# A two-layer decoder trunk on one core: up groups of the MLP in pairs, by seven block products

## The chip, the cores and the metric

The kernel runs on one core of a Trainium2 chip, in one launch. What counts is device time in microseconds (us). A time before is given as the median of three runs; the profile is a further execution, with its own time. In the profile PE is TensorE's matmuls and PEld its weight loads, DVE is VectorE, ACT ScalarE, POOL GpSimd, SP SyncE. DMAs are issued here from SP (plain loads and stores) and from POOL (loads that add to what the tile already holds, called accumulates below).

## The reference

512 tokens of width 1024 go through two layers; each has a mixer (gated linear attention in the first, stick-breaking attention in the second) and an MLP. The change concerns the MLP, whose inner width is 4096:

```python
def sq_relu_mlp(x, w_up, w_down):
    h = jax.nn.relu(x @ w_up)
    return (h * h) @ w_down

h = layer_norm(DEEPNORM_ALPHA * h + mix, ln_g[layer, 0], ln_b[layer, 0])
h = layer_norm(DEEPNORM_ALPHA * h + sq_relu_mlp(h, mlp_w_up[layer], mlp_w_down[layer]),
               ln_g[layer, 1], ln_b[layer, 1])
```

Everything is float32, in and out.

## The kernel before

**Products.** A float32 operand is split into hi and lo, two tiles of the type fp32r: hi is a copy made by ACT, lo is the operand less hi, made by the DVE (`split_tile`, L70 and L72, for weights; `put`, L98 and L99, for tokens). A product is three matmuls, hi by hi, hi by lo and lo by hi (`mm3`, L93 to L95; in the block products, L347).

**Up.** The inner width is cut into eight groups of 512. `up(g)` (L689) takes 512 of them: the weights are the stationary operand (128x128), the tokens move, 512 columns at a time, 4 banks of PSUM by 8 parts of the contraction by three, 96 matmuls. `up(0)` alone moves its tokens in two halves of 256. Its weights come in four raw pieces (512 KB each) from SP, and each piece is split. After that ACT takes the relu (L702) and the DVE (L704) or ACT (L706) the square, into a tile s2 of which there are three.

**Down.** `seven` (L292) multiplies two up groups (512 tokens by 1024) with 1024 by 1024 of the down weights, by seven block products of 2x2 blocks in place of eight. Each product takes 256 tokens, in two parts of 128 that are the stationary operand, with 12 matmuls of 512 moving columns for each part; seven products make 168. Sums and differences of blocks are needed on both sides:

- weights: four blocks in two halves each, eight tiles B (128x1024, eight buffers). b12 and b22 are sums of two blocks: a load by SP (L312), then an accumulate by POOL (L306). Two later sums, of b11 and b22 (the third), then of b21 and that (the fourth), are made by the DVE on the tiles (L371, L381), or, with `ends`, by more accumulates. Such a tile is split when a product needs it (`split_b`); the fifth product's weights come as raw pieces (`plain_b`).
- tokens: differences of blocks on the DVE, each split by `split_a`.

The products' results are added to the residual rows h by the DVE (L164, L168). The order of a down: first (b11), second (b21), third (b12), fourth (b11 with the third sum), then the product of the plain block, the seventh (b22), and the last (b21 with the fourth sum).

**Order.** `mlp` (L677) writes it by hand: up(0), up(1), affine, up(2), down(0), up(3), up(4), down(2), up(5), up(6), down(4), up(7), down(6). A scheduler then orders the rows of each engine, by its own estimates; on the chip every engine runs its rows in that order and waits where one is not ready. `affine` (L190) applies the layer norm's gain and shift to the four rows h: 16 operations of 128x512 on the DVE. A load into a tile waits until the last reader of its buffer is done; for a B tile that is the DVE's lo. There are six hi and six lo tiles for weights, three raw, and eight token units T.

Of the kernel before, what the change touches and what calls it, by code (L numbers as in the profile page):

```python
# [34 lines left out]
def yoco_kernel(ctx: ExitStack, tc: tile.TileContext, x, gla_w_in, gla_w_a2, gla_b_a, gla_norm_g,  # L35
# [22 lines left out]
    def unit(dtype):  # L58
        return big.tile([P, 4, 512], dtype, tag="T", bufs=8, name=nm("T"))
# [7 lines left out]
    def split_tile(raw, a):  # L67
        v = lambda w: w.rearrange("p (a b) -> p a b", a=a)
        hi = wts.tile([P, 1024], F32R, tag="hi", bufs=6, name=nm("hi"))
        nc.scalar.activation(hi, raw, AF.Copy)  # L70
        lo = wts.tile([P, 1024], F32R, tag="lo", bufs=6, name=nm("lo"))
# [66 lines left out]
    def lnvec(l, i):  # L138
        g = const.tile([P, D], F32, tag="lng", name=nm("lng"))
        b = const.tile([P, D], F32, tag="lnb", name=nm("lnb"))  # L140
# [144 lines left out]
    def ahead(a1, seventh=True):  # L285

        s1, s2 = (lambda u: (u[:, :, 0:256], u[:, :, 256:512]))(unit(F32))
        first = split_a(a1[:, :, 0:256])
        nc.vector.tensor_tensor(s2, a1[:, :, 0:256], a1[:, :, 256:512], op=ALU.subtract)
        return s1, s2, first, split_a(s2) if seventh else None  # L290

    def seven(a1, a2, weights, pool, hs, fresh, norms=(), mid=None, ends=False, begun=None):  # L292

# [8 lines left out]
        bs = []  # L302

        def more(b, h, k, j):

            nc.gpsimd.dma_start(out=b.rearrange("p (a b) -> p a b", a=2), in_=weights(k, h, j), accum_op=ALU.add)  # L306

        for h in range(2):
            four_b = []
            for k, j, other in ((1, 1, (0, 1)), (0, 1, (0, 0)), (0, 0, None), (1, 0, None)):  # L310
                b = pool.tile([P, 1024], F32, tag="B", bufs=8, name=nm("B"))
                nc.sync.dma_start(out=b.rearrange("p (a b) -> p a b", a=2), in_=weights(k, h, j))  # L312
                if other:
                    more(b, h, *other)
                four_b.append(b)
            bs.append(four_b)

        def split_b(i):
            got = []
            for h in range(2):  # L320
                hi, lo = split_tile(bs[h][i], 2)
                got += [(hi[:, 0, :], lo[:, 0, :]), (hi[:, 1, :], lo[:, 1, :])]
            return got

        def plain_b(k, j):
            got = []
# [647 lines left out]
```

## Time and profile before

| | |
|---|---|
| median of 3 runs | 1121.65 us (1121.54 to 1121.96) |
| profiled execution, its own time | 1122.18 us |
| its span on the core | 1120.3 us |
| granted TensorE clock, mean | 0.999 |
| one up group (512 columns) | 21.75 us (two in 43.5) |
| one down | 38.1 us (365.1 to 403.2) |
| last down, first and second layer | 40.9 us and 38.3 us |
| MLP of layer 0 | 214.5 to 547.5 us of the span |
| MLP of layer 1 | 781.7 to 1110.9 us of the span |

A row of a group reads: line, engine, operation, output from inputs by the program's names, shapes, count, then busy time in us and mean ns of one, then the idle time of that engine just before such rows. A row of the timeline starts with the start and the duration, both in us. Matmuls overlap, so that the distance of their starts, and not their duration, is what one costs. "To landing" is the time from a DMA's issue until its data are there.

### The profile page before, as it was taken

How to read it: one execution, taken by the hardware profiler on the slowest of the kernel's cores; microseconds unless marked ns; L12 is line 12 of the kernel's file. 1: busy time of each engine (PE TensorE's matmuls, PEld its weight loads, DVE VectorE, ACT ScalarE, POOL GpSimd, SP SyncE). 2: the span in 40 equal slices, each digit the busy share in tenths (PEclk: the TensorE clock that was granted, in tenths of full speed). 3: DMA queues.
4: the chain of work that ended last, by engine and by line, in shares of the span. 5: the costliest groups of instructions: out<-in, count | busy, mean ns of one | idle time of the engine just before them, and what ended most of it. 6: DMA issues, size and time to landing. Idle time of an engine off the chain costs nothing.

```text
span 1120.3 us, 14346 instructions
## 1 busy us (share of the span) xinstructions
PE 1112.0 (99%) x5519; PEld 920.9 (82%) x5519; DVE 803.9 (72%) x981; ACT 551.0 (49%) x829; POOL 168.2 (15%) x199
## 2 busy tenths in 40 slices
PE   9999999999999999999999999999999999999997
PEld 7888888898888888888888777778988888888885
DVE  4577639986856856848945888887677767667677
ACT  4455437653533534535634666664445435336353
POOL 1011222110100100122200434330200000001131
PEclk9999999999999999999999999999999999999999
DMA  8442399492670760786344221211965716706784
GB/s 248 121 132 57 117 257 215 133 285 85 189 206 25 205 202 19 204 203 137 113 113 132 57 76 39 76 38 38 295 194 149 223 42 166 229 19 187 172 133 91
DMA packets 105368, 157.52 MB, mean 141 GB/s; under 512 B 12306, under 2 KB 37266, under 8 KB 105300
## 3 DMA queue, kind: packets, MB, share of 16 engines
q1 hardware_dynamic: 87060, 120.96, 33.5%
q0 software_dynamic: 18240, 35.66, 18.6%
q8 instruction: 43, 0.70, 0.3%
q14 instruction: 25, 0.20, 0.1%
HBM read 153.45 MB, written 3.15 MB: 140 GB/s over the span
## 4 chain that ended last, share of the span: by engine, by line
PE 94%; DVE 4%; POOL 1%; issue 1%; POOLq 0%; DVEq 0%
PE ps L347 29%; PE ps L93 19%; PE ps L94 19%; PE ps L95 19%; PE ps L846 2%; PE ps L832 2%; PE ps L795 2%; POOL rs L184 1%; DVE lo L72 1%; DVE h L194 1%; DVE h L168 1%; DVE bst L175 1%; DVE T L99 0%; PE ps L567 0%; PE ps L121 0%
## 5 line engine op out<-in xcount | busy, mean ns | idle before, releaser
L347 PE MATMUL ps<-hi,T 128*128 128x512 f32 x1008 | 313.2, 390 | 0.0
L93 PE MATMUL ps<-T,hi 128*128 128x512 f32 (+1 forms) x768 | 288.5, 376 | 0.0
L94 PE MATMUL ps<-T,hi 128*128 128x512 f32 (+1 forms) x768 | 285.7, 372 | 0.1
L95 PE MATMUL ps<-T,lo 128*128 128x512 f32 (+1 forms) x768 | 285.4, 372 | 0.0
L72 DVE TENSOR_TENSOR lo<-raw,hi 128x1024 fp32r<-128x1024 f32 x134 | 162.9, 1219 | 122.8 <-ACT hi L70 122.2
L70 ACT ACTIVATE hi<-raw 128x1024 fp32r<-128x1024 f32 x134 | 141.9, 1063 | 175.7 <-PE ps L94 62.7
L347 PEld LDWEIGHTS ps<-hi,T 128*128 128x128 f32 x1008 | 188.9, 188 | 39.9 <-DVE T L99 1.0
L72 DVE TENSOR_TENSOR lo<-B,hi 128x1024 fp32r<-128x1024 f32 x108 | 131.1, 1221 | 99.8 <-ACT hi L70 99.7
L347 PE MATMUL ps<-lo,T 128*128 128x512 f32 x504 | 196.2, 389 | 0.0
L70 ACT ACTIVATE hi<-B 128x1024 fp32r<-128x1024 f32 x108 | 114.2, 1059 | 162.1 <-PE ps L94 106.3
L95 PEld LDWEIGHTS ps<-T,lo 128*128 128x128 f32 x768 | 144.7, 188 | 25.2
L93 PEld LDWEIGHTS ps<-T,hi 128*128 128x128 f32 x768 | 144.6, 188 | 24.5 <-issue 0.9
L94 PEld LDWEIGHTS ps<-T,hi 128*128 128x128 f32 x768 | 144.8, 189 | 23.9 <-DVE T L99 0.3
L306 POOL DMA_DIRECT2D B<-in_mlp_w_down_dram x52 | 62.4, 1234 | 540.9 <-DMA B<-in_mlp_w_down_dram 451.6
L347 PEld LDWEIGHTS ps<-lo,T 128*128 128x128 f32 x504 | 94.7, 188 | 19.5
L93 PE MATMUL ps<-hi,T 128*128 128x512 f32 x256 | 102.3, 400 | 0.0
L95 PE MATMUL ps<-hi,T 128*128 128x512 f32 x256 | 100.1, 391 | 0.0
L94 PE MATMUL ps<-lo,T 128*128 128x512 f32 x256 | 100.1, 391 | 0.0
L168 DVE TENSOR_TENSOR h<-h,ps 128x512 f32<-128x512 f32 x110 | 74.7, 680 | 6.0 <-PE ps L95 3.6
L823 POOL TENSOR_TENSOR w<-w,r 128x512 f32<-128x512 f32 x32 | 53.0, 1658 | 132.9 <-DVE r L822 125.0
L822 DVE TENSOR_TENSOR_SCAN r<-r,begin 128x512 f32<-128x512 f32 x40 | 65.9, 1651 | 2.7 <-ACT r L819 2.2
L95 PEld LDWEIGHTS ps<-hi,T 128*128 128x128 f32 x256 | 48.1, 188 | 10.5 <-DVE T L99 0.2
(179 smaller groups left out, 1163.0 us busy)
## 6 DMA issues: line engine op xcount, KB each, us to landing
raw<-in_mlp_w_up_dram SPq DMA_DIRECT2D x64, 512.0 KB, 5.4
B<-in_mlp_w_down_dram SPq DMA_DIRECT2D x64, 512.0 KB, 5.8
B<-in_mlp_w_down_dram POOLq DMA_DIRECT2D x52, 512.0 KB, 8.1
raw<-in_gla_w_in_dram SPq DMA_DIRECT2D x20, 512.0 KB, 3.7
raw<-in_mlp_w_down_dram SPq DMA_DIRECT2D x16, 512.0 KB, 4.7
raw<-in_kv_w_dram SPq DMA_DIRECT2D x16, 512.0 KB, 4.0
B<-in_gla_w_o_dram POOLq DMA_DIRECT2D x14, 512.0 KB, 7.9
B<-in_gla_w_o_dram SPq DMA_DIRECT2D x8, 512.0 KB, 5.8
```

The source lines that it names most:

```text
L70: nc.scalar.activation(hi, raw, AF.Copy)
L72: nc.vector.tensor_tensor(lo, raw, hi.bitcast(F32), op=ALU.subtract)
L93: nc.tensor.matmul(ps, lhsT=a[0], rhs=b[0], start=first, stop=False)
L94: nc.tensor.matmul(ps, lhsT=a[0], rhs=b[1], start=False, stop=False)
L95: nc.tensor.matmul(ps, lhsT=a[1], rhs=b[0], start=False, stop=last)
L168: nc.vector.tensor_tensor(h, h, ps, op=op)
L306: nc.gpsimd.dma_start(out=b.rearrange("p (a b) -> p a b", a=2), in_=weights(k, h, j), accum_op=ALU.add)
L347: nc.tensor.matmul(banks[s], lhsT=a(k, s)[x], rhs=b[k][y], start=opens and (k, x, y) == (0, 0, 0), stop=closes and (k, x, y) == (3, 1, 0), ...
L795: nc.tensor.matmul(zs[b + a][:, at], lhsT=self.q[x][own, P * i:P * i + P], rhs=self.k[y][own, 0:n], start=(x + y == 0), stop=(x == 1), ski ...
L822: nc.vector.tensor_tensor_scan(down, down, begins[kind][:, ::-1], 1.0, op0=ALU.mult, op1=ALU.max)
L823: (nc.vector if kind == 2 else nc.gpsimd).tensor_tensor(w, w, r[:, 1:S + 1], op=ALU.mult)
L832: nc.tensor.transpose(out=ps[:, P * b:P * b + P], in_=w[:, P * b:P * b + P], identity=ident)
```

## The change

1. In each layer groups 2 and 3, 4 and 5, 6 and 7 are computed in pairs by `up_seven`, also by seven block products in place of eight: 7 products of 48 matmuls, each with 128x128 of weights stationary and 256 columns (half the tokens) moving. That makes 336 matmuls of 256 columns for 192 of 512. Groups 0 and 1 stay as they were.
2. The weights of such a pair are handled by a class `Blocks`, shared with the downs: eight B tiles, four of them with an accumulate, two DVE sums for the third and two for the fourth. The blocks are now loaded in the order b11, b21, b12, b22, both halves of each.
3. The token operands of `up_seven` are the same for the three pairs of a layer: `token_sums` makes them once a layer, on ACT and the DVE, from the hi and lo that exist. T has ten buffers, not eight; hi and lo have five, not six.
4. Results of `up_seven` lie in PSUM banks of two 256-column halves. Some products' results are kept by an ACT copy and then added to by the DVE (L792), followed by relu and square on ACT.
5. The order becomes up(0), up(1), affine and token sums, down(0), up_seven(2), down(2), up_seven(4), down(4), up_seven(6), down(6): from there on, downs and pairs of ups alternate. The layer norm's vectors lie in an s2 tile, no longer in constant tiles, and the affine rows are written behind up(1).
6. In a down, two token differences are made in place, and the seventh product's in a raw tile.

The matmuls of the whole program go from 5397 to 6261 rows: 128x512 from 4276 to 3124, 128x256 from 552 to 2568. DVE rows go from 983 to 1059, ACT rows from 811 to 939, SP's loads and stores from 257 to 269, POOL's accumulates from 66 to 90.

```diff
-        return big.tile([P, 4, 512], dtype, tag="T", bufs=8, name=nm("T"))
+        return big.tile([P, 4, 512], dtype, tag="T", bufs=10, name=nm("T"))
...
-        hi = wts.tile([P, 1024], F32R, tag="hi", bufs=6, name=nm("hi"))
+        hi = wts.tile([P, 1024], F32R, tag="hi", bufs=5, name=nm("hi"))
...
+    class Blocks:
+        def __init__(self, weights, pool):
+            self.weights, self.bs = weights, [[None] * 4 for _ in range(2)]
+            for i, k, j, other in ((2, 0, 0, None), (3, 1, 0, None), (1, 0, 1, (0, 0)), (0, 1, 1, (0, 1))):
+                for four_b, h in zip(self.bs, range(2)):
+                    b = pool.tile([P, 1024], F32, tag="B", bufs=8, name=nm("B"))
+                    nc.sync.dma_start(out=b.rearrange("p (a b) -> p a b", a=2), in_=weights(k, h, j))
+                    if other:
+                        self.more(b, h, *other)
+                    four_b[i] = b
...
+        def third_sum(self, ends):
+            for h, (b22, b12, b11, b21) in enumerate(self.bs):
+                if ends:
+                    self.more(b11, h, 0, 1)
+                    self.more(b11, h, 1, 1)
+                else:
+                    nc.vector.tensor_tensor(b11, b22, b11, op=ALU.add)
...
+        def token_sums():
+            (h0, h1), (l0, l1) = hT.hi, hT.lo
...
+            def less(out, ah, al, bh, bl):
+                part = quarter()
+                tt(part, al, bl, op=ALU.subtract)
+                tt(out, ah, bh, op=ALU.subtract)
+                tt(out, out, part, op=ALU.add)
...
+        def up_seven(g, tokens):
+            w = Blocks(lambda k, h, j: block(mlp_w_up[l], 512 * k + 256 * h, 512 * (g + j)), mlp_)
+            first, second, third, fourth, third_, seventh, fourth_ = tokens
...
+            def part(s, a, b, banks, opens, closes):
+                if opens:
+                    banks[s] = bank()
+                for f in (2 * s, 2 * s + 1):
+                    at = banks[s][:, 256 * (f % 2):256 * (f % 2) + 256]
+                    for k in range(4):
+                        for x, y in ((0, 0), (0, 1), (1, 0)):
+                            nc.tensor.matmul(at, lhsT=b[k][x][:, 128 * f:128 * f + 128], rhs=a(k)[y],
...
+            product(first, w.split(2), ys, True, False, keep, 0, 0)
+            product(second, w.split(3), xs, True, True, close, 0, 0)
+            w.third_sum(False)
+            product(third, w.split(1), zs, True, False, keep, 1, 1)
+            w.fourth_sum(False)
+            product(fourth, w.split(2), ys, False, False, keep, 0, 1)
+            product(third_, w.plain(1, 1), zs, False, True, close, 0, 1)
+            product(seventh, w.split(0), ys, False, False, close, 1, 1)
+            product(fourth_, w.split(3), ys, False, True, close, 1, 0, True)
+            return out
...
         sq = [up(0), up(1)]
+        vec = four()
+        vec = lnvec(*lacks, *(vec[:, 2 * i:2 * i + 2, :].rearrange("p a b -> p (a b)") for i in range(2)))
         for h in hs:
             h.affine(vec)
+        tokens = token_sums()
         for g in range(0, NG - 2, 2):
-            sq.append(up(g + 2))
             for _ in down(g):
                 pass
-            if g < NG - 4:
-                sq.append(up(g + 3))
...
+            sq = up_seven(g + 2, tokens)
+        steps = down(NG - 2, norms=range(NT) if l == 0 else (2, 3), ends=True)
```

How the rows of the DVE move, at three places. Names: h302 to h305 are the residual rows, ps are PSUM banks, lng and lnb the norm's vectors, raw and B weights as loaded, T token operands.

The first place is the affine of layer 0. Before, on the DVE, its rows stand between the token lo's that up(0) waits for:

```order
L194 TENSOR_TENSOR h303_1642<-h303_1642,lng306_1649 128x512 x2
L99 TENSOR_TENSOR T311_1658<-s2410_2171,T310_1657 128x4x128
L194 TENSOR_TENSOR h303_1642<-h303_1642,lnb307_1650 128x512 x2
L99 TENSOR_TENSOR T313_1660<-s2412_2183,T312_1659 128x4x128
L194 TENSOR_TENSOR h304_1643<-h304_1643,lng306_1649 128x512 x2
L194 TENSOR_TENSOR h304_1643<-h304_1643,lnb307_1650 128x512 x2
```

After, on the DVE, where up(1) ends and the first down starts (s2429 is up(1)'s output, s2430 holds the norm's vectors, ps451 and ps452 are the first product's banks, T453 the lo of the second product's token operand):

```order
L192 TENSOR_TENSOR h302_1641<-h302_1641,s2430_2465 128x512 x3
L719 TENSOR_TENSOR s2429_2456<-ps428_2359,s2429_2456 128x512
L192 TENSOR_TENSOR h302_1641<-h302_1641,s2430_2465 128x512
L192 TENSOR_TENSOR h303_1642<-h303_1642,s2430_2465 128x512 x4
L192 TENSOR_TENSOR h304_1643<-h304_1643,s2430_2465 128x512 x4
L192 TENSOR_TENSOR h305_1644<-h305_1644,s2430_2465 128x512 x4
L164 SCALAR_TENSOR_TENSOR h302_1641<-h302_1641,ps451_2541 128x512
L164 SCALAR_TENSOR_TENSOR h303_1642<-h303_1642,ps452_2555 128x512
L99 TENSOR_TENSOR T453_2569<-s2429_2456,T453_2569 128x4x256
```

The 16 rows moved from up(0) to the end of up(1): 13 of them now stand behind the last relu multiply (L719) and ahead of T453's lo.

The second place is the weights' third sums. Before, on the DVE ahead of the second down of layer 0, they stand among the relu multiplies of an up group (B535 and B539 are b22's two halves, B537 and B541 b11's):

```order
L72 TENSOR_TENSOR lo547_3212<-B537_3188,hi546_3210 128x1024
L704 TENSOR_TENSOR s2517_3040<-ps513_2940,s2517_3040 128x512
L371 TENSOR_TENSOR B537_3188<-B535_3182,B537_3188 128x1024
L704 TENSOR_TENSOR s2517_3040<-ps514_2941,s2517_3040 128x512
L704 TENSOR_TENSOR s2517_3040<-ps515_2942,s2517_3040 128x512
L72 TENSOR_TENSOR lo549_3216<-B541_3198,hi548_3214 128x1024
L704 TENSOR_TENSOR s2517_3040<-ps516_2943,s2517_3040 128x512
L371 TENSOR_TENSOR B541_3198<-B539_3192,B541_3198 128x1024
```

After, on the DVE, from the end of down(4) of layer 0 into up_seven(6) (B685 and B686 are the halves of b11, B687 and B688 of b21, B691 and B692 of b22, the last two with an accumulate each; lo702 and lo704 are the second product's weights):

```order
L72 TENSOR_TENSOR lo696_4338<-B685_4314,hi695_4336 128x1024
L72 TENSOR_TENSOR lo698_4342<-B686_4316,hi697_4340 128x1024
L166 TENSOR_TENSOR h305_1644<-h305_1644,ps648_4063 128x512
L72 TENSOR_TENSOR lo702_4398<-B687_4318,hi701_4396 128x1024
L166 TENSOR_TENSOR h304_1643<-h304_1643,ps647_4049 128x512
L318 TENSOR_TENSOR B685_4314<-B691_4328,B685_4314 128x1024
L318 TENSOR_TENSOR B686_4316<-B692_4331,B686_4316 128x1024
L166 TENSOR_TENSOR h305_1644<-h305_1644,ps648_4063 128x512
L72 TENSOR_TENSOR lo704_4402<-B688_4320,hi703_4400 128x1024
```

The sums (L318) stand ahead of lo704, the second half of the second product's weights, and behind the last down product's adds.

The third place is the way from up_seven(4) into down(4) of layer 0, after, on the DVE (B633 and B634 are the halves of the down's b11, B639 of its b22, s2596 the second group's output, ps601 and ps602 the banks of the seventh product):

```order
L72 TENSOR_TENSOR lo632_3962<-B590_3566,hi631_3960 128x1024
L72 TENSOR_TENSOR lo644_4043<-B633_4016,hi643_4041 128x1024
L792 TENSOR_TENSOR s2596_3581<-s2596_3581,ps601_3590 128x2x256
L99 TENSOR_TENSOR T649_4077<-s2596_3581,T649_4077 128x4x256
L318 TENSOR_TENSOR B633_4016<-B639_4030,B633_4016 128x1024
L792 TENSOR_TENSOR s2596_3581<-s2596_3581,ps602_3616 128x2x256
L72 TENSOR_TENSOR lo646_4047<-B634_4018,hi645_4045 128x1024
```

The first half's sum stands ahead of the add (L792) that reads ps602; the last product of up_seven writes into that bank again.

More of the change, by code (lines that the diff above doesn't have):

```diff
@@ L301, in seven @@
         a11, a21, a12, a22 = a1[:, :, lo_t], a1[:, :, hi_t], a2[:, :, lo_t], a2[:, :, hi_t]
[L302 to L326, printed above, removed]
[L327 to L330 removed]
+        w = Blocks(weights, pool)
+        split_b, plain_b = w.split, w.plain
         seen = set()
```

155 lines of the change are left out of this document (102 added, 53 removed).

## The prediction

> **What bounds the kernel now.** First the head of the page: busy times and the engine shares of the chain of work that ended last.
>
> ```profile
> span 1120.3 us, 14346 instructions
> PE 1112.0 (99%) x5519; PEld 920.9 (82%) x5519; DVE 803.9 (72%) x981; ACT 551.0 (49%) x829; POOL 168.2 (15%) x199
> PE 94%; DVE 4%; POOL 1%; issue 1%; POOLq 0%; DVEq 0%
> ```
>
> TensorE is busy 99% of the span and carries 94% of the chain. The waits of PE say whether anything holds it:
>
> ```profile
> PE ps L443 <- POOL ident L131: 1.6, 1, 1.6
> PE ps L229 <- DVE h L188: 0.7, 2, 0.4
> ```
>
> These are its two largest waits, 2.3 us together, and neither lies in the MLP. So time goes only by shortening PE's work, and every new wait costs in full. The windows that matter are an opening stretch of up(0), two up groups together, one down, and the last down of each layer.
>
> ```profile
> core 0: us, PE busy (x) PEld busy (x) DVE busy (x) ACT busy (x) POOL busy (x), PEclk, DMA share, GB/s
> 214.60:220.20 5.60, 5.60 (x48) 5.54 (x47) 5.48 (x11) 3.38 (x4) 0.54 (x1) 1.00 0.54 177
> 321.60:365.10 43.50, 43.50 (x193) 36.05 (x192) 27.44 (x28) 15.06 (x18) 0.00 (x0) 1.00 0.25 73
> 365.10:403.20 38.10, 38.10 (x169) 31.54 (x169) 29.01 (x32) 18.09 (x18) 4.77 (x4) 1.00 0.82 219
> 506.60:547.50 40.90, 40.47 (x186) 33.00 (x185) 38.85 (x50) 25.62 (x39) 7.45 (x7) 1.00 0.55 120
> 1072.60:1110.90 38.30, 38.30 (x170) 31.49 (x169) 34.16 (x43) 21.80 (x26) 9.21 (x10) 1.00 0.50 79
> ```
>
> Two up groups take 43.5 us with the DMA engines at a quarter; a down takes 38.1 with them at 0.82. The slack in which a down's weights are loaded, summed and split is thus the 43.5 us of matmuls that ask little of the DMA engines. What the second row's loads waited for, in the waits of SP's queue:
>
> ```profile
> SPq L312 <- DVE lo L72: 268.8, 48, 26.8
> ```
>
> Loads of B start when the lo of a slot's last reader is done, 48 times, up to 26.8 us after the queue came to them. The DVE's order therefore sets when the next transfer starts.
>
> **PE's gain.** Matmul starts of the timeline, 256 columns and 512, and the weight loads of the 214.6 window:
>
> ```profile
> 215.77 0.28 PE L94 MATMUL ps<-T,hi 128*128 128x256 f32 x1
> 215.89 0.28 PE L95 MATMUL ps<-T,lo 128*128 128x256 f32 x1
> 330.46 0.39 PE L93 MATMUL ps<-T,hi 128*128 128x512 f32 x1
> 330.68 0.39 PE L94 MATMUL ps<-T,hi 128*128 128x512 f32 x1
> L94 PEld LDWEIGHTS ps<-T,hi 128*128 128x128 f32 x16 | 3.1, 191 | 0.1
> ```
>
> A pair of up groups is 192 matmuls of 512 columns: 43.50 / 192 = 0.2266 us each. In its place come 7 x 48 = 336 of 256 columns. The starts stand 0.12 us apart, though a weight load lasts 0.191: loads overlap, and nothing but issue sets the step. So the pair becomes 336 x 0.120 = 40.3, a gain of 3.18 us, and six pairs give **-19.1**. The rows hold 48 such matmuls in 5.60 us, 0.117 each, so the gain could reach 25 by that average; I take 0.120 since the timeline has it matmul by matmul.
>
> The Trainium skill, "TensorE: Matmul & The Clock Gate", section Back-to-back issue gap, gives N/2.4 + 2.5 ns for a lone stream, 109 and 216 ns here, and by it the gain would be 6 x (41.4 - 36.7) = 28.4; it says itself that at small N weight loads make it longer, and the trace, with 120, agrees with that warning.
>
> **The first down of each layer.** The 16 affine multiplies and adds move from the DVE's slack in up(0) to a place where 13 of them stand behind the last relu multiply of up(1) and ahead of the second product's token lo. Their price, and that of an ACT relu, an add and a lo:
>
> ```profile
> 228.36 1.29 DVE L194 TENSOR_TENSOR h<-h,lnb 128x512 f32<-128x512 f32 x2
> 229.56 0.68 DVE L99 TENSOR_TENSOR T<-s,T 128x512 fp32r<-128x512 f32 x1
> 382.29 2.35 DVE L72 TENSOR_TENSOR lo<-B,hi 128x1024 fp32r<-128x1024 f32 x2
> 384.56 0.68 DVE L168 TENSOR_TENSOR h<-h,ps 128x512 f32<-128x512 f32 x1
> 385.16 1.22 DVE L99 TENSOR_TENSOR T<-s,T 128x1024 fp32r<-128x1024 f32 x1
> 444.22 0.60 ACT L702 ACTIVATE s<-ps 128x512 f32<-128x512 f32 x1
> ```
>
> Two affines take 229.56 - 228.36 = 1.20 us, so 0.60 each; an add 0.60 (385.16 - 384.56); a lo 1.13 ((384.56 - 382.29) / 2). From the end of up(1): relu 0.60, multiply 0.60, 13 affines 7.8, two adds 1.2, lo 1.13: done at 11.3, and about 0.6 of hand-overs between engines makes 11.9 (an estimate: four hand-overs at some 0.15). PE has only the first product, 38.1 / 7 = 5.44 us, and two matmuls of the second, 0.45. It stands **6.0 us, twice: +12.0**. Without the affines the lo would be done at 4.1, in time. No cover is left here: up(2), which lay between in the kernel before, has gone.
>
> **From a down to the next up by seven, three times a layer.** Up by seven needs eight B tiles, four of them with an accumulate DMA; they go into the slots that the down frees. What such transfers take, alone and in company (issues, first and last start, and times to landing):
>
> ```profile
> L312 SPq DMA_DIRECT2D B<-in_mlp_w_down_dram x1: 368/368/368, 362.1 to 362.1; - x1
> DMA to landing us min/median/max: 3.5/3.5/3.5
> L306 POOL DMA_DIRECT2D B<-in_mlp_w_down_dram x3: 1187/1198/1689, 494.3 to 497.7; - x3
> DMA to landing us min/median/max: 5.9/6.0/8.1
> L306 POOL DMA_DIRECT2D B<-in_mlp_w_down_dram x2: 1185/1192/1198, 469.6 to 471.4; - x2
> DMA to landing us min/median/max: 7.9/9.0/10.1
> L312 SPq DMA_DIRECT2D B<-in_mlp_w_down_dram x3: 367/368/368, 466.3 to 471.4; - x3
> DMA to landing us min/median/max: 4.6/7.0/9.3
> ```
>
> A load alone takes 3.5, beside others 4.6 to 9.3. An accumulate takes 5.9 with little beside it; three land from about 500.2 to 497.7 + 8.1 = 505.8, so 2.8 apart. Beside loads it takes 7.9 to 10.1, and two land at 477.5 and 481.5, 4.0 apart.
>
> Count from the down's start. Its fourth product ends at 4 x 5.44 = 21.8. The DVE then does an add (22.4), a lo of a raw piece (23.5), the lo's of the two b22 halves (24.7, 25.8), a token lo (26.9), and the lo's of the b21 halves (28.1, 29.2). Only the four at 24.7 to 29.2 free the slots that up's b12 and b22 wait for. At best the first accumulate lands at 24.8 + 3.5 + 5.9 = 34.2, the fourth 3 x 2.8 later, 42.6, which is 4.5 into up by seven (the down ends at 38.1). Both third sums, which wait for the third and fourth accumulate, stand in the DVE's order ahead of one residual add and the lo of the second product's second half: 4.5 + 1.13 + 0.60 + 1.13 = 7.4. PE comes to it after one product and its first half tile's share, 48 x 0.120 + 6 x 0.120 = 6.5. The least stall is 0.9. Beside three loads and a raw piece I take 4.6 for the load, 7.9 for the first accumulate, and 2.9 apart after that, since by then no loads are left: 46.0, so 7.9 + 2.86 - 6.5 = 4.3. At 4.0 apart it is 7.6. **Six times 4.3: +25.8** (5.4 to 45.6). In the kernel before, the sums lay far ahead of their use:
>
> ```profile
> 422.35 1.22 DVE L371 TENSOR_TENSOR B<-B,B 128x1024 f32<-128x1024 f32 x1
> 427.79 1.22 DVE L371 TENSOR_TENSOR B<-B,B 128x1024 f32<-128x1024 f32 x1
> ```
>
> Their down began at 446.7, 19 to 24 us later (the second 38.1 us stretch behind 365.1 and 43.5 of ups: 365.1 + 38.1 + 43.5).
>
> **From up by seven to the next down, four with sums on the DVE.** The slots come free at 20.0, 24.7, 25.9 and 30.7 of up's clock, at the lo's behind its fourth to sixth product. The first down sum waits for the third accumulate and stands ahead of the add that reads the seventh product's second bank; PE writes into that bank again at 6.5 x 5.76 = 37.4. At best: 24.7 + 3.5 + 5.9 + 2.8 = 36.9, sum and add 1.73, 38.6: 1.2 late. With 4.6 and 7.9: 4.3. The loads lie wider apart than above, so I take the middle, **2.8 x 4 = +11.2** (4.8 to 17.2).
>
> **Smaller terms.** The delayed sums push the lo's of a down's third product: 0 to 1.9 each, 1.0 taken, **+4** for four downs. The last down of each layer fills its sums by 14 accumulates, 14 x 2.8 = 39 us against a down of 38 to 41 that starts with few of them landed: 0 to 4 each, **+3** for both. The token halves' sums cost nothing while they stay in up(1): between its start and its end the DVE now has 2 multiplies and 17 operations of 1024 columns, 1.2 + 19.2 = 20.4 us of 43.5 / 2 = 21.8; two of the 17 are sums that wait for an accumulate, and where that is late the 1.4 us left are gone, so 0 to 3 each, 0 taken. Five hi and lo tiles for six outside the MLP: 0, hidden by a lead of some 3 us of products; 0 to 4 if that lead is gone. The DVE as a whole is no bound: 27.4 + 29.0 = 56.4 us of a pair's 81.6 become 56.4 + 6 lo's and 4 sums at 1.13, less 2 of the 8 multiplies at 0.60, about 67 of 78.4.
>
> **Sum.** -19.1 + 12.0 + 25.8 + 11.2 + 4 + 3 = +36.9. The profiled execution took 1122.18 us, 1.9 more than its span and 0.5 above the median of the runs; 1122.2 + 36.9 = **1159**. With every unknown at its least: -19.1 + 12.0 + 5.4 + 4.8 = +3.1, 1125. At its most: -19.1 + 12.0 + 45.6 + 17.2 + 7.6 + 8 + 6 + 4 = +81, 1203.
>
> **Rivals.**
> 1. Nothing is held: transfers land early, the DVE's order is not what decides, 1122.2 - 19.1 = 1103, faster. For it: PE hardly waited before, with the same tiles and DMAs. Against: the 43.5 us with the DMA engines at 0.25 are gone, and the affines alone take back 12.
> 2. Only the affines and the least stalls: 1125, within 1119 to 1138. It decides if accumulates land 2.8 apart and loads in 3.5 throughout. For: the DMA share of a pair would be only (0.25 x 43.5 + 0.82 x 38.1) / 81.6 = 0.52, plus the added 6 transfers. Against: bursts, as at 466 to 482.
> 3. The stalls slow the matmuls behind them as well. Cold matmuls are in the opening rows:
>
> ```profile
> 1.59 2.18 PE L443 MATMUL ps<-ident 128*128 128x128 f32 x9 [1.59 <-POOL ident L131]
> 4.49 2.34 PE L460 MATMUL ps<-ident 128*128 128x128 f32 x10
> 6.63 1.06 PE L121 MATMUL ps<-ident,h 128*128 128x128 f32 x4
> 7.48 0.71 PE L460 MATMUL ps<-ident 128*128 128x128 f32 x4
> ```
>
> At first ten start in 6.63 - 4.49 = 2.14, 214 ns each; from 7.48 it is half of that. From 1.59 to 7.48 PE ran at half speed: 2.95 us lost. If each of the eight long stalls (six before an up's second product, two in a first down) ended so, 8 x 2.95 = 23.6: 1183, slower still. It decides where stalls pass the length that cools PE; no wait in this trace is that long. The Trainium skill, same page, Part 1 on the clock gate, sets that at an idle window of about 3.4 us and asks for no gaps over some 3 us between bursts: a rule that speaks against this change if the stalls are as long as I think.
>
> That the change doesn't do what it says is ruled out by the order of instructions: 336 matmuls stand where 192 stood.
>
> **Chances.** A measurement of this kernel can tell about 0.2%, 2.2 us. The forecast, 1138 to 1203, 0.58; nothing held, 0.12; the least stalls, 0.18, of which 0.06 within 1119.4 to 1123.9; cooling on top, 0.12. Faster 0.12, same 0.06, slower 0.82. The range 1117 to 1203 leaves out the first rival and a part of the last.
>
> **What would show it.** In the profile of the changed kernel: matmuls 0.120 apart in an up by seven; PE waits behind a DVE lo in its second product, about 4 us, six times; about 6 us in each first down behind a token lo; DVE waits for a DMA at the third sums; spans of 40.3 + 4 and of 38.1 + 3. Wrong: PE busy 99% again, or waits at other places, or matmuls at 0.2 us behind each stall (then rival 3).

## The result, and the profile after

The changed kernel takes 1243.45 us in the median of four runs (1236.84 to 1246.06), the kernel before 1121.66: a ratio of 1.107, interval 1.1052 to 1.1089. It is slower, as forecast, but by 122 us and not by 37, above the range. Its four runs lie 9 us apart, so single runs below are read by their stages more than by their totals. The head of the page of after, with busy times and the engine shares of the chain that ended last:

```profile
span 1243.4 us, 16445 instructions
PE 1130.5 (91%) x6383; PEld 972.8 (78%) x6383; DVE 897.2 (72%) x1057; ACT 640.4 (52%) x957; POOL 198.4 (16%) x223
PE 54%; DMA 21%; DVE 15%; issue 7%; POOL 1%; ACT 1%; SPq 0%; POOLq 0%; DVEq 0%; ACTq 0%
```

PE was on 94% of the chain and is now on 54%; DMAs and the DVE have most of the rest. PE is busy 18.5 us longer although its work got shorter, which already says that some of its matmuls run slowly. What PE waits for, in the waits of after (total, times, longest):

```profile
PE ps L775 <- DVE s L792: 32.4, 4, 8.3
PE ps L775 <- DVE lo L72: 25.7, 6, 4.8
PE ps L373 <- ACT T L98: 23.6, 3, 10.4
PE ps L373 <- DVE T L99: 14.8, 3, 7.9
```

The four rows are, in order, the last products of four ups by seven, the second products of all six, the last downs with one place in a first down, and the first downs with one short wait in the attention's output product. The stages, in windows of after: first down, an up by seven, a middle down, the last down (layer 0), then first and last down of layer 1.

```profile
core 0: us, PE busy (x) PEld busy (x) DVE busy (x) ACT busy (x) POOL busy (x), PEclk, DMA share, GB/s
267.30:314.70 47.40, 41.09 (x169) 33.32 (x168) 44.68 (x54) 21.26 (x22) 3.57 (x3) 0.93 0.45 126
314.70:371.30 56.60, 44.37 (x337) 43.93 (x336) 31.36 (x30) 27.69 (x36) 5.96 (x5) 0.88 0.63 155
371.30:409.60 38.30, 38.30 (x170) 31.49 (x169) 35.56 (x37) 20.79 (x22) 3.57 (x3) 1.00 0.55 156
552.50:609.20 56.70, 44.71 (x193) 35.80 (x192) 41.06 (x52) 26.34 (x39) 12.37 (x12) 0.88 0.78 149
889.50:940.60 51.10, 40.36 (x169) 32.40 (x169) 49.19 (x58) 24.56 (x27) 3.58 (x3) 0.90 0.42 117
1179.90:1232.90 53.00, 40.99 (x171) 32.34 (x170) 35.55 (x42) 22.96 (x28) 13.91 (x12) 0.90 0.76 141
```

The up by seven takes 56.6 us, of which PE is busy 44.4, not 40.3; its granted clock is 0.88, where it was 1.00 everywhere in the MLP before. The middle down has no wait at all. The six ups by seven take 56.6, 57.4, 47.1, 58.5, 57.3 and 46.8, in all 323.8 for 261.0 of the twelve up groups before (+62.8). The first downs add 47.4 + 51.1 - 2 x 38.1 = 22.3, the last 56.7 - 40.9 + 53.0 - 38.3 = 30.5, and the attention's output product ahead of the first MLP 5.3 (up(0) starts at 219.8, not 214.5). The four middle downs add 0.8 and the rest 1.4: together 123.1, the difference of the two spans.

How one such wait comes about, in after: the DVE's rows and PE's at the end of the first up by seven (the bracket is the idle time before a row and what ended it).

```profile
364.41 1.23 DVE L318 TENSOR_TENSOR B<-B,B 128x1024 f32<-128x1024 f32 x1 [10.03 <-DMA B<-in_mlp_w_down_dram]
365.55 0.68 DVE L792 TENSOR_TENSOR s<-s,ps 128x512 f32<-128x512 f32 x1
```

```profile
366.28 0.80 PE L775 MATMUL ps<-T,hi 128*128 128x256 f32 x2 [8.01 <-DVE s L792]
```

The DVE is idle for 10.0 us with the sum (L318) at its head, which waits for an accumulate; the add (L792) behind it had all it needs, and PE waits 8.0 us for that add. The other stall of this up, in its second product, and the matmuls behind it:

```profile
325.82 0.39 PE L775 MATMUL ps<-T,lo 128*128 128x256 f32 x1 [4.22 <-DVE lo L72]
327.28 0.41 PE L775 MATMUL ps<-T,lo 128*128 128x256 f32 x1
327.49 0.63 PE L775 MATMUL ps<-T,hi 128*128 128x256 f32 x2
```

The rows at 327.28 and 327.49 start 0.21 us apart; from 330.1 on it is 0.12 again. Summed over the trace, matmuls that start this late cost 22.1 us in the six ups, 3.4 in the first downs and 2.8 in the last.

The transfers behind that first sum, issues (first and last start) and times to landing of the down's loads, accumulates and plain pieces, and the window in which they run:

```profile
L302 SPq DMA_DIRECT2D B<-in_mlp_w_down_dram x4: 368/368/368, 341.7 to 351.5; - x4
DMA to landing us min/median/max: 3.4/3.7/8.5
L309 POOL DMA_DIRECT2D B<-in_mlp_w_down_dram x4: 1185/1192/1198, 345.7 to 359.7; - x4
DMA to landing us min/median/max: 7.2/8.6/9.4
L64 SPq DMA_DIRECT2D raw<-in_mlp_w_down_dram x2: 526/548/569, 351.9 to 352.6; - x2
DMA to landing us min/median/max: 8.5/9.8/11.1
341.70:366.90 25.20, 17.19 (x142) 16.99 (x141) 10.31 (x11) 11.88 (x15) 4.77 (x4) 0.88 0.83 209
```

The accumulates take 7.2 to 9.4 us and one load 8.5: a burst with the DMA engines at 0.83. Two plain pieces of 512 KB for the down's fifth product, which ACT reads some 20 us after they land, run in the middle of it.

### The profile page after: what moved, and what is told of

Read it like the earlier page. It is cut to its first block, busy times and chain, and to the rows that moved or that the text cites. A ratio compares the mean times of both kernels' runs of the same rounds, so it can differ in the third digit from the quotient of the medians.

```text
span 1243.4 us, 16445 instructions
## 1 busy us (share of the span) xinstructions
PE 1130.5 (91%) x6383; PEld 972.8 (78%) x6383; DVE 897.2 (72%) x1057; ACT 640.4 (52%) x957; POOL 198.4 (16%) x223
## 3 DMA queue, kind: packets, MB, share of 16 engines
q0 software_dynamic: 24768, 48.24, 22.4%
## 4 chain that ended last, share of the span: by engine, by line
PE 54%; DMA 21%; DVE 15%; issue 7%; POOL 1%; ACT 1%; SPq 0%; POOLq 0%; DVEq 0%; ACTq 0%
PE ps L775 12%; DMA B<-in_mlp_w_down_dram 10%; PE ps L93 9%; PE ps L94 9%; PE ps L95 9%; PE ps L373 8%; DMA B<-in_mlp_w_up_dram 8%; DVE lo L72 6%; DVE T L99 3%; DMA B<-in_gla_w_o_dram 3%; PE ps L948 1%; DVE h L192 1%; DVE h L166 1%; PE ps L934 1%; PE ps L897 1%
## 5 line engine op out<-in xcount | busy, mean ns | idle before, releaser
L373 PE MATMUL ps<-hi,T 128*128 128x512 f32 x1008 | 322.9, 399 | 42.3 <-ACT T L98 23.6
L775 PE MATMUL ps<-T,hi 128*128 128x256 f32 x1344 | 262.6, 298 | 32.4 <-DVE s L792 32.4
L70 ACT ACTIVATE hi<-B 128x1024 fp32r<-128x1024 f32 x180 | 188.7, 1056 | 167.5 <-PE ps L373 84.8
L373 PEld LDWEIGHTS ps<-hi,T 128*128 128x128 f32 x1008 | 192.9, 192 | 88.4 <-ACT T L98 24.8
L775 PEld LDWEIGHTS ps<-T,hi 128*128 128x128 f32 x1344 | 226.8, 206 | 33.7 <-DVE s L792 33.2
L72 DVE TENSOR_TENSOR lo<-B,hi 128x1024 fp32r<-128x1024 f32 x180 | 215.2, 1220 | 41.4 <-ACT hi L70 41.3
L775 PE MATMUL ps<-T,lo 128*128 128x256 f32 x672 | 200.8, 299 | 25.7 <-DVE lo L72 25.7
L72 DVE TENSOR_TENSOR lo<-raw,hi 128x1024 fp32r<-128x1024 f32 x98 | 119.2, 1218 | 57.9 <-ACT hi L70 56.7
L775 PEld LDWEIGHTS ps<-T,lo 128*128 128x128 f32 x672 | 138.9, 207 | 26.9 <-DVE lo L72 26.9
L93 PE MATMUL ps<-T,hi 128*128 128x512 f32 (+1 forms) x384 | 139.1, 363 | 0.1
L94 PE MATMUL ps<-T,hi 128*128 128x512 f32 (+1 forms) x384 | 136.2, 355 | 0.5 <-DVE T L99 0.5
L95 PE MATMUL ps<-T,lo 128*128 128x512 f32 (+1 forms) x384 | 136.0, 354 | 0.0
L318 DVE TENSOR_TENSOR B<-B,B 128x1024 f32<-128x1024 f32 x24 | 29.4, 1223 | 97.2 <-DMA B<-in_mlp_w_up_dram 52.1
L99 DVE TENSOR_TENSOR T<-s,T 128x1024 fp32r<-128x1024 f32 (+1 forms) x58 | 65.5, 1129 | 36.9 <-ACT T L98 36.9
L95 PEld LDWEIGHTS ps<-T,lo 128*128 128x128 f32 x384 | 72.6, 189 | 10.2
```

The source lines that it names most:

```text
L72: nc.vector.tensor_tensor(lo, raw, hi.bitcast(F32), op=ALU.subtract)
L93: nc.tensor.matmul(ps, lhsT=a[0], rhs=b[0], start=first, stop=False)
L94: nc.tensor.matmul(ps, lhsT=a[0], rhs=b[1], start=False, stop=False)
L95: nc.tensor.matmul(ps, lhsT=a[1], rhs=b[0], start=False, stop=last)
L99: keep(nc.vector.tensor_tensor(lo, ps, hi.bitcast(F32), op=ALU.subtract))
L318: nc.vector.tensor_tensor(b11, b22, b11, op=ALU.add)
```

## The experiments

My theory (A): the DVE runs its rows in order, and the sums that wait for accumulates stand ahead of rows that PE needs; a PE that idles long enough then runs at half speed for a while. The main rival (B): the transfers themselves are too slow for this order of stages, so that the waits would only move.

**Sums later.** With a fixed order on the DVE, the third sums are put behind the lo of the third product's weights, in `seven` (without `ends`) and in `up_seven`:

```diff
-        w.third_sum(ends)
         product(*second, xs, True, True, 0, 0, last=True)
+        if not ends:
+            with tc.issue_after(behind.ins):
+                w.third_sum(ends)
...
-            w.third_sum(False)
             product(third, w.split(1), zs, True, False, keep, 1, 1)
+            with tc.issue_after(newest[0].ins):
+                w.third_sum(False)
```

> The third sums of the weights are ordered on VectorE behind the lo's of the third product's weights, in the downs and in the ups by seven; nothing else changes. Theory A (the sums wait for the accumulates and hold up what stands behind them on VectorE): the six stalls of 4.4 us in an up's second product and the four of 8.3 us before its last product's second bank go, 26.6 + 33.1 us, and with them the half-speed matmuls behind them, 22 us in all; up to 15 us may come back at the third or fourth product. Time 1160 to 1180. Rival B (the weights themselves land late, the transfers are the bound): the stalls move on to the third and fourth product, at most 20 us go, time above 1220.

1179.77 us, 1.052 times before (1.0495 to 1.0544): 63.7 us of the 121.8 go. Two windows of this kernel, a middle down and the up by seven behind it, under the columns above:

```profile
361.00:404.20 43.20, 40.75 (x171) 32.49 (x170) 39.04 (x41) 20.59 (x22) 4.89 (x5) 0.96 0.65 173
404.20:444.50 40.30, 40.30 (x338) 40.30 (x337) 27.61 (x27) 27.46 (x36) 3.83 (x5) 1.00 0.69 174
```

Every up by seven now takes 40.3 us, with no wait and full clock: the gain on PE is there in full, and the same transfers are in time for where their data are really needed. B falls. The middle downs give back 3.3 to 4.9 us each, in waits for lo's that now come late, and the total lies at the upper end of A's 1160 to 1180.

**A stall filled.** 34 transposes that nobody uses stand ahead of each second product of an up by seven:

```diff
+            spare = bank()
+            for _ in range(34):
+                nc.tensor.transpose(out=spare[:, :P], in_=ident, identity=ident)
             product(second, w.split(3), xs, True, True, close, 0, 0)
```

> 34 transposes of the identity into a spare bank are added ahead of each second product of an up by seven; they give nothing that is used. They take 34 x 0.109 = 3.7 us of the 4.4 us in which TensorE stands there. Theory A (an idle TensorE slows down, and that is a cost of its own): the wait left is under 1 us, the matmuls behind it start 0.12 us apart and not 0.21, six times 2.0 us go, 12 us in all: about 1231. Rival C (the matmuls behind the stall are slow for another reason, such as weights that still come in): they stay at 0.21, the time stays at 1243 or gets longer.

1229.63 us (one run): 14 us less for 204 more instructions on PE. The six ups take 306.3 us, transposes included, for 323.8. PE's rows in the first such place of this kernel:

```profile
322.47 3.87 PE L804 MATMUL ps<-ident 128*128 128x128 f32 x34
327.51 0.39 PE L775 MATMUL ps<-T,lo 128*128 128x256 f32 x1 [0.21 <-DVE lo L72]
327.73 0.40 PE L775 MATMUL ps<-T,hi 128*128 128x256 f32 x2
327.97 0.28 PE L775 MATMUL ps<-T,lo 128*128 128x256 f32 x1
```

The matmuls behind stand 0.12 us apart (three in 327.73 to 328.09), not 0.21. So the idle time itself, and not what comes in behind it, makes them slow: the prediction's third rival, at about 2 us a stall. The Trainium skill, "TensorE: Matmul & The Clock Gate", Part 1 on the clock gate, lets the clock halve after an idle window of about 3.4 us and rise again after about as long a busy one. The way up agrees roughly: the slow stretches of the changed kernel's matmuls lasted 3 to 6 us. The idle time that it takes does not come out as one length. PE's rows behind 2.45 us of idle time, in the kernel of the last run below, and behind 4.13 us, in the kernel with the affine early:

```profile
363.63 0.73 PE L774 MATMUL ps<-T,hi 128*128 128x256 f32 x2 [2.45 <-DVE s L791]
364.16 0.41 PE L774 MATMUL ps<-T,lo 128*128 128x256 f32 x1
364.37 0.63 PE L774 MATMUL ps<-T,hi 128*128 128x256 f32 x2
```

```profile
1133.75 0.38 PE L775 MATMUL ps<-T,lo 128*128 128x256 f32 x1 [4.13 <-DVE lo L72]
1133.97 0.40 PE L775 MATMUL ps<-T,hi 128*128 128x256 f32 x2
1134.20 0.28 PE L775 MATMUL ps<-T,lo 128*128 128x256 f32 x1
```

Behind the shorter wait the matmuls stand 0.21 us apart at once, with a granted clock of 0.50 from 363.7 to 367.1. Behind the longer one they stand 0.12 apart for 1 us, and 0.21 only after that. So a wait of a few us risks half speed, and no run here gives a length below which it is safe.

**The affine early.** The vectors are loaded first, and the 16 rows written between up(0) and up(1):

```diff
-        sq = [up(0), up(1)]
         vec = four()
...
+        sq = [up(0)]
         for h in hs:
             h.affine(vec)
+        sq.append(up(1))
```

> The layer norm's vectors are loaded before up(0), and the affine rows are written between up(0) and up(1); nothing else changes. Theory A: the stall in the second product of the first down goes in layer 0 (6.5 us and 2.2 us of slow matmuls); in layer 1, where the token sums also wait for accumulates, 9.6 us of affine go from an 11.4 us stall, and 1.2 us of slow matmuls if what is left is under 3 us. Sum about 18, time about 1225. Rival D (the token sums and not the affine are what is late): at most 5 us go.

1232.06 us (one run), 11.4 less: between theory A's 18 and rival D's 5. The first downs take 41.0 and 47.1 us (47.4 and 51.1), 10.4 off, but the first down of layer 0 starts at 270.8, not 267.3. The affine was the larger part of that stall in layer 0; 9 us of it stay in layer 1. There, after, the DVE's rows and PE's:

```profile
894.39 1.89 DVE L192 TENSOR_TENSOR h<-h,s 128x512 f32<-128x512 f32 x3
896.20 0.68 DVE L719 TENSOR_TENSOR s<-ps,s 128x512 f32<-128x512 f32 x1
896.80 7.91 DVE L192 TENSOR_TENSOR h<-h,s 128x512 f32<-128x512 f32 x13
...
905.82 1.22 DVE L99 TENSOR_TENSOR T<-s,T 128x1024 fp32r<-128x1024 f32 x1
```

```profile
898.02 0.50 PE L373 MATMUL ps<-hi,T 128*128 128x512 f32 x1 [2.87 <-ACT T L98]
907.09 1.22 PE L373 MATMUL ps<-hi,T 128*128 128x512 f32 x2 [7.87 <-DVE T L99]
```

The rows are those of the order: three affines, the last relu multiply, thirteen affines, two adds, the lo. But the multiply comes at 896.2, 6.7 us after the end of up(1) at 889.5, where the working had 0.6: the token sums had run over, since the two weight sums among them waited 1.1 and 3.4 us for DMAs. PE thus waits twice.

**The plain pieces behind the accumulates.** The fifth product's two pieces are loaded from POOL's queue:

```diff
-                hi, lo = split_piece(self.weights(k, h, j), 2)
+                hi, lo = split_piece(self.weights(k, h, j), 2, nc.gpsimd)
```

> The two plain pieces of each fifth product are loaded from the queue that issues the accumulates, so that in a down they come behind its four accumulates; nothing else changes. Theory E (the stall before the last product of an up by seven is 8.3 us and not 2.8 because those two pieces, 1 MB at 209 GB/s, 5 us, share the burst): the third accumulate lands 4 to 5 us sooner, the four stalls shrink from 8.3 to about 4, and the slow matmuls behind them get fewer: 16 to 24 us, time 1219 to 1227. Rival F (the accumulates are slow by themselves, one after another): the stalls stay within 1 us of 8.3, the time within 5 us of 1243.

1240.21 us (one run), as near to 1243 as F gave it. The four stalls shrink from 8.1 to 5.6 us on average (32.4 and 22.4 in all), which is neither E's 4 nor F's 8.3, and the six ups take 310.3 us, 13.5 less; the last downs take 10 more, since there the pieces come behind fourteen accumulates. The total says little, as the edit moved two things; the landings say more. In after, the third accumulate of these four downs lands 5.3 to 6.6 us behind the second (358.4 and 364.3 in the first), here 2.7 to 4.2. So the two pieces make up about half of what the stall has over my 2.8. The other half is there without them: in both kernels the second accumulate lands within 1 us of the moment at which PE comes to the bank, where the middle of the working had it some 1.7 us ahead.

**The last downs' sums on the DVE,** by `ends` left at its default there:

```diff
-        steps = down(NG - 2, norms=range(NT) if l == 0 else (2, 3), ends=True)
+        steps = down(NG - 2, norms=range(NT) if l == 0 else (2, 3))
```

> The last down of each layer makes its third and fourth sums on VectorE, as the other downs do, and not by ten further accumulates; nothing else changes. Theory G (fourteen accumulates in a row, 2.8 us each, are what that down waits for): its stalls, about 10.7 us and some smaller ones, go in both layers, 26 us with the slow matmuls; but the third sum then stands on VectorE ahead of the last up's last product, as in the other pairs, and 8.3 + 2 us come back there in each layer. Net -3 to -12, time 1231 to 1240. Rival H (the order of the loads, b11 and b21 first, makes the accumulates start late, however the sums are made): the stall in the last down stays at some 10 us and 20 us come on top: time above 1255.

1242.74 us (one run). The last up by seven of layer 0 and the last down of layer 1, windows of this kernel:

```profile
507.80:563.90 56.10, 44.60 (x337) 44.15 (x337) 31.47 (x31) 27.77 (x36) 5.96 (x5) 0.88 0.61 154
1189.30:1227.60 38.30, 38.30 (x170) 31.46 (x169) 36.77 (x43) 23.11 (x28) 3.42 (x3) 1.00 0.09 28
```

Both halves of theory G show: the last down is back at 38.3 us (53.0), and the last up has the stall that the others have (56.1 for 47.1). They cancel nearly, and the total was 3 us above what I gave, less than the spread of the changed kernel's runs. Why the last down waits is seen in ACT's rows of after:

```profile
576.43 1.06 ACT L70 ACTIVATE hi<-B 128x1024 fp32r<-128x1024 f32 x1 [7.63 <-DMA B<-in_mlp_w_down_dram]
...
578.34 1.04 ACT L98 ACTIVATE T<-s 128x1024 fp32r<-128x1024 f32 x1
```

ACT stands 7.6 us for a block that still gets an accumulate, and the token hi that PE wants is two rows behind it: the same pattern, on ACT.

**The old load order where `ends`.** b22 and b12 first, half by half, for the output product and the last downs:

```diff
+            if ends:
+                order = (order[3], order[2], order[0], order[1])
+                pairs = [(o, h) for h in range(2) for o in order]
```

> Where sums are made by accumulates (the last downs and the attention's output product) the blocks are loaded in the order of the kernel before, b22 and b12 first, half by half; nothing else changes. Rival H: the output product before the first MLP gets its 5.3 us back and the last downs 13 to 15 us each, time about 1212. Theory G: the output product gets up to 5 us back, the last downs stay within 3 us of 56.7 and 53, since the accumulates are bound by their own rate and by slots that come free late: time 1236 to 1243.

1234.5 us (one run), 9 less and outside both expectations. The last downs get about 6 us each back, of 14 to 16, and the output product nothing (its last accumulate lands at 205.0, as in after, where it was 194.4 before). So the order of the loads is a part for the last downs, and not the cause at the output product.

**Five hi and lo tiles alone,** in the kernel before:

```diff
-        hi = wts.tile([P, 1024], F32R, tag="hi", bufs=6, name=nm("hi"))
+        hi = wts.tile([P, 1024], F32R, tag="hi", bufs=5, name=nm("hi"))
```

(and the same for lo, and where `trio` is made).

> The kernel before with five hi and five lo tiles for weights, not six; nothing else changes. Theory J (the five tiles cost nothing outside the MLP, as the prediction took; the 5.3 us before the first up come from elsewhere in the change): within 2 us of 1122. Rival K (they are what makes the output product before the first MLP later): 4 to 10 us slower, its product ends by some 5 us later.

1136.15 us, 1.0131 times before (1.0116 to 1.0146): the smallest-looking line of the change costs 14 us by itself, more than K's 4 to 10. Its trace loses 4.8 us by the start of the first down (288.3 for 283.5), 4.8 more across the last down of layer 0, and the rest at the end of layer 1: the three block products whose sums are accumulates. POOL's waits, of before and then of this kernel:

```profile
POOL B L306 <- DVE lo L72: 69.7, 13, 16.0
```

```profile
POOL B L306 <- DVE lo L72: 195.8, 12, 50.1
```

An accumulate onto a block that has been split already waits for that split's lo; with one pair of tiles less the lo's come later, and the output product's last accumulate lands at 203.6, not 194.4.

**All parts together.** Third sums as above, fourth sums behind the fifth product's weights, the affine early, the old load order where `ends`; the last downs' sums on the DVE in the first run, by accumulates in the second:

```diff
+        if not ends:
+            with tc.issue_after(newest[0].ins):
+                w.fourth_sum(ends)
+        p7 = seventh, split_b(0)
```

> Together: third sums behind the third product's weights, fourth sums behind the fifth product's weights (VectorE), the affine early, the last downs' sums on VectorE, the old load order where accumulates make the sums. Theory A, with each part's share: 1180 for the later sums, 11 off for the affine, 3.5 us off for each of four middle downs (14), 26 off for the last downs, 5 off for the output product: about 1124, between 1112 and 1140. If the ups by seven keep 40.3 us and every wait is gone the floor is 1103. Rival I (the transfers or VectorE as a whole are then the bound): above 1150.

> As the run with all parts, but the last downs make their sums by accumulates. Theory G: 10 to 25 us longer than that run. Rival H: within 4 us of it, or shorter.

1138.09 us (1.0137, 1.012 to 1.0155) and 1148.36 us (1.0242, 1.0221 to 1.0264). Theory A's sum of parts gave 1124 and at most 1140, so the first run is inside, 14 us above the sum; rival I falls, and G's 10 us between the two holds.

**The affine on GpSimd,** on top of the first of them:

```diff
-            h.affine(vec)
+            h.affine(vec, nc.gpsimd)
```

> The run with all parts and VectorE sums (1138), with the MLP's 16 affine rows moved from VectorE to GpSimd, 16 x 1.66 = 26.5 us there beside up(0) and up(1). Theory L (VectorE is full in up(0) and up(1): 16 affine rows and 25 rows of token sums on top of the splits; this makes the 3 to 4 us by which these two ups are longer): 3 to 10 us faster, 1128 to 1135. Rival M (it was not VectorE, or GpSimd's accumulates behind the affine rows come late): within 2 us of 1138, or slower.

1155.08 us (1.0285, 1.0262 to 1.0307): 17 us slower. That is rival M's side, by more than either expectation had in mind. The group of the 16 rows on POOL, and rows of the DVE at the same time, of this kernel:

```profile
L194 POOL TENSOR_TENSOR h<-h,s 128x512 f32<-128x512 f32 x16 | 32.3, 2060 | 3.3 <-DMA s<-in_ln_g_dram 3.3
```

```profile
239.26 2.31 DVE L759 TENSOR_TENSOR T<-T,T 128x1024 f32<-128x1024 f32 x1
241.49 2.31 DVE L74 TENSOR_TENSOR lo<-raw,hi 128x1024 fp32r<-128x1024 f32 x1
```

While POOL runs them, a DVE operation of 1024 columns with two inputs takes 2.2 to 2.3 us, where it takes 1.22: the affine left the DVE and made the others of this kind there nearly twice as long. The Trainium skill, "SBUF — State Buffer", section SBUF: two separate sides, says that the two engines share a pair of ports that one instruction holds for its whole length. That the two slow each other agrees: POOL's rows took 2.06 us each, where its rows of the same shape take 1.66 in the kernel before. The full length does not come out: 1.22 and 1.66 one after the other would make 2.88, not 2.31.

Rival M's other reason is in the trace as well: the first down's four accumulates stand behind the 16 rows and start at 262.9 us, not at 243.1. The first downs are 7.8 and 2.3 us longer than in the run that this one builds on, 10 of the 17 us; how they divide between the two causes no run shows.

**Six tiles again.** The first run with all parts, with six hi and lo tiles, nine T units, and the seventh product's token operand split late (the tiles by the reverse of the edit above); and, alone, the changed kernel with those three edits and nothing else:

```diff
-        return big.tile([P, 4, 512], dtype, tag="T", bufs=10, name=nm("T"))
+        return big.tile([P, 4, 512], dtype, tag="T", bufs=9, name=nm("T"))
...
-        seventh = seventh()
...
-        p7 = seventh, split_b(0)
+        p7 = seventh(), split_b(0)
```

> The run with all parts and VectorE sums (1138), with six hi and six lo tiles again; the room comes from nine T units, not ten, and so that these are enough the seventh product's token operand is split late in each block product. Theory K (what that run still has over the kernel before is the five tiles, 14 us there, at three places where a layer's product hands over): 10 to 16 us faster, 1122 to 1128; with the gain of the matmuls left in part it may pass below 1122. Rival N (nine T units make the downs wait, or VectorE is full): 1132 to 1150.

> The changed kernel with six hi and six lo tiles, nine T units and the late split of the seventh token operand; the sums stand where they stood. Theory A: the stalls behind the third sums stay (26 + 33 us and the slow matmuls), only the 14 us of the three hand-overs go, less what the other waits swallow: 1225 to 1240. Rival O (the five tiles are behind the large stalls too): below 1200.

1121.05 us for all parts (ratio 0.999, 0.9981 to 0.9999) and 1230.56 us (one run) for the change with six tiles. The three edits together are worth 17 and 13 us, near what K and A gave. But the second run does not confirm A's account of where the time lies, since its waits have moved. PE's waits in it, and the DVE's rows at the end of its first middle down:

```profile
PE ps L373 <- DVE h L166: 42.4, 6, 7.5
PE ps L774 <- DVE s L791: 11.5, 4, 3.6
```

```profile
408.94 1.22 DVE L318 TENSOR_TENSOR B<-B,B 128x1024 f32<-128x1024 f32 x1 [8.87 <-DMA B<-in_mlp_w_up_dram]
410.08 0.68 DVE L166 TENSOR_TENSOR h<-h,ps 128x512 f32<-128x512 f32 x1
```

The third sum of the next up now stands ahead of a residual add at the end of the down, and PE waits 6.8 to 7.5 us for that add, six times; the waits in the second products are gone, and those ahead of the last products fell from 32.4 to 11.5 us. The mechanism is the same, a sum that holds a row behind it, at a place that the scheduler chose anew. So the 13 us are not the tiles' alone.

The version with all parts and six tiles takes the same time as the kernel before, within the 0.2% that a measurement can tell. The busy line of its page, and then one whole pair, up by seven and down:

```profile
PE 1097.1 (98%) x6383; PEld 946.7 (85%) x6383; DVE 904.0 (81%) x1065; ACT 631.0 (57%) x957; POOL 175.8 (16%) x203
```

```profile
300.90:379.70 78.80, 78.66 (x505) 71.87 (x504) 66.89 (x68) 46.87 (x57) 8.72 (x8) 1.00 0.72 187
```

PE's work is 14.9 us shorter than before (1112.0), and the pair is at 78.8 us, for 81.6 before and 78.4 in the working. Most of what is missing of the 19 us lies outside the pairs: from the start of the last down of layer 0 to the mixer's long row of products behind it 60.5 us pass, for 53.4 before, and the tail behind the last matmuls of the MLP takes 12.1 us for 9.4; the rest are smaller waits at the hand-overs.

## Why the prediction was right and wrong

| step | prediction | measured |
|---|---|---|
| matmuls, six pairs | -19.1 | -19.2 (40.3 for 43.5 each, with the sums later) |
| second products of the ups | +25.8 | +25.7 |
| last products of the ups | +11.2 | +32.4 |
| first downs | +12.0 | +18.9, and 3.4 of slow matmuls |
| lo's in the middle downs | +4 | +0.8 |
| last downs | +3 | +27.7, and 2.8 of slow matmuls |
| five tiles outside the MLP | 0 | +5.3 (a part of the last downs beside it) |
| slow matmuls behind stalls | 0; 23.6 as a rival | +28.3, of which 22.1 in the ups |

- The direction, the place and the mechanism of the main loss were right: the sums ahead of what PE needs, on the DVE. Moved, they give 64 us back. The size was missed by more than a factor of three.
- The second products came out to 0.1 us. The working went row by row through the order, with the durations of transfers that run beside others. That close a match is partly luck: the accumulates landed 2.5 us apart and not 2.9, and the first of them about as much later as this saved.
- The step that failed for the last products is "The loads lie wider apart than above, so I take the middle". The plain pieces come into the same stretch, which I had counted for the way into an up and not for the way into a down. Loads and accumulates took the upper durations (8.5, 7.2 to 9.4): the second accumulate landed where the upper case had it, and the third 5.3 to 6.6 us behind it, for the 2.8 of the working. The term came out at 32.4 us, not 11.2.
- The step that failed for the last downs is "0 to 4 each". I had multiplied 14 accumulates by 2.8 us and compared the total with a down, and not asked when the block of the fourth product is complete, and who stands behind it. With the sums on the DVE the last down of layer 1 takes 38.3 us, so the accumulates are the cause. An ACT row that waits for one holds the token hi; the new load order, which starts the accumulates later, makes 6 us of each, and the five tiles a part (4.8 us across the last down of layer 0 in the kernel before).
- The step that failed for the slow matmuls is that they were left out of the sum. The third rival had a chance of 0.12, and it decided 28 us: 14 waits of 3.9 to 10.4 us, some 2 us on top of each, for 8 waits at 2.95 in its own count. Once I forecast waits over 4 us, it was no rival but their consequence: the opening rows had shown both speeds.
- Five tiles were put at 0 "hidden by a lead of some 3 us". They cost 14 us in the kernel before. I had looked for readers that wait, and not for accumulates that wait for the readers.
- In the first downs the affine cost what was worked out in layer 0 (a wait of 6.3 us, for 6.0); in layer 1 the token sums, put at 0 of 3 us, were some 6 late.
- Two slips of the working change nothing: the wait at L229 lies inside the span of the first MLP (0.3 us at 223.1 and 0.4 at 541.7), and 6 x (41.4 - 36.7) is 28.2.

Not settled: how the excess of the last downs divides between the load order, the five tiles and the accumulates themselves, and why layer 1 keeps 9 us in its first down with the affine early, where PE still waits 0.9 and 3.1 us for token rows and 1.8 for a weight's lo.

## What to carry to other kernels

A queue that runs in order makes a row that waits for a transfer hold all rows behind it: with every new sum, ask not when its data land but what stands behind it, and place it just ahead of its first use. A wait of a few us on TensorE can cost more than itself, here some 2 us for waits of 3.9 to 10.4, and should stand in the sum from the start. After an edit, look where the waits are and not only at the time: with six tiles the time came out as forecast while the waits had moved. One buffer less can delay transfers that wait for that buffer's readers, far from the line where it was taken.

## What was not expected of the hardware

- Two-input VectorE operations of 1024 columns take 2.2 to 2.3 us instead of 1.22 while GpSimd runs operations on SBUF of its own (16 rows, 32.3 us).
- Matmuls ran at half speed at once behind 2.45 us of idle time, and at full speed for another 1 us behind 4.13; filling the idle time with unused transposes made the kernel 14 us faster.
- In the changed kernel's burst an accumulate took up to 9.4 us and a plain load 8.5, with the DMA engines busy 0.83 and 209 GB/s moved; alone they had taken 5.9 and 3.5.
